# Three groups of mixer steps traced one to three steps later in a decoder layer on one core

## The chip, the cores and the metric

The kernel runs on one core of a Trainium2 chip. The metric is the device time of one execution in microseconds (us); of several executions the median is taken. The engines are TensorE (PE, with its weight loads as PEld), VectorE (DVE), ScalarE (ACT), GpSimd (POOL), and SyncE (SP), whose queue issues the weight loads from memory.

## What is computed

One decoder layer in float32 for 256 tokens of width 2048. A feed-forward block comes first and last; between them stand the mixer, which this document is about, and a cross-attention into 256 memory vectors. The mixer of the reference, cut to what matters:

```python
h = rms_norm(x, norm_g)
p = h @ w_in
q, k, v, p_rwkv, gates = jnp.split(p, c, axis=-1)
y_attn = sliding_window_attention(q, k, v, sinks)          # 16 heads, 4 key heads of 64
y_rwkv = rwkv7_time_mix(p_rwkv, ...)                       # 16 heads of 64, a scan over time
gate_attn, gate_rwkv = jnp.split(jax.nn.sigmoid(gates), 2, axis=-1)
merged = gate_attn * (y_attn @ w_proj_attn) + gate_rwkv * (y_rwkv @ w_proj_rwkv)
return x + merged @ w_out
```

and in `rwkv7_time_mix` the two sigmoids over 1024 columns that the change concerns:

```python
w_log = -softplus(-(w0 + jnp.tanh(xw) @ w2)) - 0.5
a = jax.nn.sigmoid(a0 + xa @ a2)
```

## The kernel before

**Products.** Every weight matrix is read once, in units of 256 rows by up to 512 columns. Each unit is split on ACT (L299, the high part) and DVE (L300, the rest), and a product of 256 tokens with it is three matmuls for every 128 rows of the matrix and every 128 tokens (`multiply`, L336 to L338). `product` (L312) walks through the units of one column block; units are loaded by SP's queue (L287) four units ahead and split two units ahead.

**Steps.** All other work of the mixer consists of Python generators that are put into queues (`Interleave`, L51 on: "const", "feat", "attn", "ew", "chain", "norm", "mem"). After the six matmuls of one unit for one half of the tokens, `product` calls `bg.tick()` (L324), and a tick advances the first task of every queue by one `yield` (two tasks in "attn", three in "chain"). So a `yield` is the unit of distance: a piece of work behind it is traced one step, which is six product matmuls, later. `idle(n)` yields n times. A task that needs another's result waits, step by step, until a name is put into `bg.seen`. A product whose left operand isn't traced yet goes on ticking without matmuls (L320). The tile framework then makes each engine's order out of the traced order, and puts in the waits; each engine works its queue in that order.

**Around the change.** The products of the mixer follow one another: queries (two blocks), keys and values, the small columns (288 wide), the RWKV keys (two), four times gate and attention projection, receptances and values (two of each), four gates, four blocks of the RWKV projection, four of the output product.

- `keys_values` (L515 on): transposes the keys (L347), copies them to `kd` (L521), and moves one half of them to the other partitions by two DMAs on POOL's queue (L522). Next step: the values are copied (L525). After `idle(2)` the name "kv" is seen. The eight `attend` tasks wait for it, two at a time; the first thing they do is the scores (L542) from `kd`, into two of the three PSUM banks named `mm`. The last one lets "attn" be seen.
- `decay_and_rate` (L644 on) waits for "attn". It loads `wa` on POOL's queue (L648, L649), and then, in four groups, makes four matmuls each (L661; the profile shows two records for each, 32 in all) into two `mm` banks, and four sigmoids on ACT (L668), with a `yield` between groups. Then come scans and exponentials, and "decay" is seen. Behind it in the same queue "ew" stand `removal_keys` for two halves (L717, L754 on PE), `substitute` (a loop of 31 small DVE steps; its input `dl` is read by SP's queue, L775), and `receptances` and `values` for two halves (L835, L843). These set off the `pair` tasks of the queue "chain" (L893 to L960), and those the `finish` tasks (L985, L994), which split the second branch into `yr`.
- `merged` (L1033 on): after each block of the RWKV projection, DVE multiplies the gate in (L1045) and POOL adds the two branches (L1046), one instruction for each half of the tokens, into `ml`. The task then waits one `yield`, transposes `ml` on PE (L347, two groups of four) and splits it (L352, L353) into the left operand `mt` of the output product.

Large tiles of the mixer share a ring of 20 buffers (`t4`); the PSUM has three banks for products (`acc`), three `mm` and two `tr`.

Of the kernel before, what the change touches and what calls it, by code (L numbers as in the profile page):

```python
# [120 lines left out]
def decoder_layer(ctx: ExitStack, tc: tile.TileContext, a: dict, out: bass.AP):  # L121
# [24 lines left out]
    def mm():  # L146
        return ps.tile([P, 512], F32, tag="mm", name="mm")
# [4 lines left out]
    def wait_for(name):  # L152
        while name not in bg.seen:
            yield

    def idle(n):
        for _ in range(n):
            yield
# [181 lines left out]
    def feat(tok, cols):  # L340


        b = tr()
        for i, col in enumerate(cols):
            for t in range(2):
                o = (2 * i + t) * P
                pe.transpose(b[:, o : o + P], tok[:, t, col : col + P], ident[:])  # L347
        return b[:].rearrange("p (c t) -> p c t", c=2)

    def split(x: Act, c, n, src):  # L350

        act.copy(x.at(0, c, n), src)  # L352
        dve.tensor_tensor(x.at(1, c, n), src, f32(x.at(0, c, n)), ALU.subtract)  # L353
        x.done |= set(range(c, c + n))
# [124 lines left out]
    with tc.tile_pool(name="mx", bufs=1, reuse_waits="tile") as sp:  # L479
        aligned(sp)  # L480

        def t4(name, shape=(P, 4, T), dt=F32):
            return sp.tile(list(shape), dt, tag="t4", name=name, bufs=N4)
# [31 lines left out]
        def keys_values():  # L515

            b = feat(tok_kv, C4[:2])
            v = kd[:].rearrange("p (c e) t -> p c e t", e=2)
            for e in range(2):
                r, o = slice(64 * e, 64 * e + 64), slice(64 - 64 * e, 128 - 64 * e)  # L520
                act.copy(v[r, :, e, :], b[r])  # L521
                pool.dma_start(v[o, :, e, :], v[r, :, e, :])  # L522
            yield
            for t in range(2):
                dve.tensor_copy(vt[:, t, :], tok_kv[:, t, KV_W : 2 * KV_W])  # L525
            yield from idle(2)
            bg.seen.add("kv")

        bg.spawn("feat", keys_values())
        ya = act_tiles("ya", 2)  # L530
        sink4 = sinks[:].rearrange("p (k c e) -> p k e c", k=4, c=2)
# [101 lines left out]
        def halves(x):  # L633
            return x[:].rearrange("p c (b t) -> p (c b) t", b=2)
# [9 lines left out]
        def decay_and_rate():  # L644
            yield from wait_for("small")
            yield from wait_for("attn")
            wa = t4("wa", (P, RW))
            pool.dma_start(wa[0:64, :], W["rwkv_w2"])  # L648
            pool.dma_start(wa[64:128, :], W["rwkv_a2"])  # L649
            act.activation(xwa[0:64, :], xwa[0:64, :], AF.Tanh)  # L650
            act.activation(xg, xg, AF.Sigmoid)
            yield
            for h in range(2):
                cs.append(t4("cs"))
                aa.append(t4("aa"))
                for q in (0, 2):
                    b = [mm() for _ in range(2)]
                    for i in range(2):
                        for e in range(2):
                            r, c = slice(64 * e, 64 * e + 64), (4 * h + q + i) * P  # L660
                            pe.matmul(  # L661
                                b[e][:, i * T : (i + 1) * T], wa[r, c : c + P], xwa[r, :],
                                start=True, stop=True,
                            )
                    for i in range(2):
                        for e, (dst, bias) in enumerate(((cs[h], w0), (aa[h], a0))):
                            c = 4 * h + q + i
                            act.activation(  # L668
                                dst[:, q + i, :], b[e][:, i * T : (i + 1) * T], AF.Sigmoid,
                                bias=bias[:, c : c + 1],  # L670
                            )
                    yield
            for h in range(2):
                for c in range(4):
                    dve.tensor_tensor_scan(
                        cs[h][:, c, :], keep2, cs[h][:, c, :], 0.0, ALU.mult, ALU.add
                    )
                    if c % 2:
                        yield
                c3 = halves(cs[h])  # L680
                mid = stat.tile([P, 8], F32, tag="mid", name="mid")
                dve.tensor_copy(mid[:], c3[:, :, 63])
                dve.tensor_tensor(
                    c3, c3, mid[:].unsqueeze(2).to_broadcast([P, 8, P]), ALU.subtract
                )
                dec.append(stat.tile([P, 4], F32, tag="dec", name="dec"))
                dve.tensor_tensor(dec[h][:], cs[h][:, :, 127], mid[:, 1:8:2], ALU.add)
                yield
                act.activation(dec[h][:], dec[h][:], AF.Exp, scale=-DECAY)

                ee.append(t4("ee", (P, 8, P)))
                e0.append(stat.tile([P, 8], F32, tag="e0", name="e0"))
                act.activation(e0[h][:], mid[:], AF.Exp, scale=DECAY)
                act.activation(ee[h][:], c3, AF.Exp, scale=-DECAY)
                yield
                act.activation(cs[h][:], cs[h][:], AF.Exp, scale=DECAY)
                yield
            bg.seen.add("decay")

        bg.spawn("ew", decay_and_rate())  # L700
        kt = []

# [328 lines left out]
        mt = act_tiles("mt", 4)  # L1031

        def merged(m, n):  # L1033
            yield
            for q in (0, 2):
                split(mt, 4 * n + q, 2, feat(m, C4[q : q + 2]))
                yield

        for n in range(4):
            g, m = t4("gl", (P, 2, 512)), t4("ml", (P, 2, 512))  # L1040
            pool.dma_start(g[:], blk(grd, n))
            pool.dma_start(m[:], blk(md, n))
            pr = product(yr, W["w_proj_rwkv"])
            for t in range(2):
                dve.tensor_tensor(g[:, t, :], pr[t][:], g[:, t, :], ALU.mult)  # L1045
                pool.tensor_tensor(m[:, t, :], g[:, t, :], m[:, t, :], ALU.add)  # L1046
            bg.spawn("feat", merged(m, n))
# [166 lines left out]
```

## Time and profile before

| what | value |
|---|---|
| median of 3 runs (lowest, highest) | 2328.53 us (2326.44, 2334.17) |
| the profiled execution | 2327.99 us |
| its span, first to last instruction | 2326.3 us |
| mean granted TensorE clock | 0.998 |
| PE busy in 700 to 800 us | 100.00 of 100 |
| PE busy in 800 to 900 us | 97.34 of 100, clock 0.98 |
| PE busy in 900 to 1000 us | 99.72 of 100 |
| PE busy in 1300 to 1400 us | 96.80 of 100 |
| DVE busy, whole span | 1259.5 us |
| ACT busy, whole span | 1078.2 us |

The mixer runs from about 754 us to 1600 us. The keys' task is found at 816 us, the sigmoids at 879 to 889, the sum of the branches at 1350 to 1396. A wait is shown as the idle time of an engine before an instruction, together with what released it.

### The profile page before, as it was taken

To read this page: it belongs to the slowest core of one execution; us is meant where nothing else is said; L and a number is where in the kernel's file an instruction comes from. 1 tells how busy PE (TensorE), PEld (TensorE's weight loads), DVE (VectorE), ACT (ScalarE), POOL (GpSimd) and SP (SyncE) were. 2 spreads that over 40 slices of the span, in tenths; PEclk is the share of its full clock that TensorE was granted. 3 is DMA by queue.
4 is the path that set the end of the run, shared out by engine and by line. 5 is a ranking of instruction groups with operands and counts; after the bars stand their busy time and mean duration, and the time that the engine had idled before them with its cause. 6 is when DMAs were issued, how large, how long until landed. Compare 5 with 4: busy or idle time off the path is not lost.

```text
span 2326.3 us, 27347 instructions
## 1 busy us (share of the span) xinstructions
PE 2303.9 (99%) x10853; PEld 1895.5 (81%) x10853; DVE 1259.5 (54%) x1395; ACT 1078.2 (46%) x1425; POOL 130.3 (6%) x192
## 2 busy tenths in 40 slices
PE   8999999999999999999999999999999999999998
PEld 7888888888888877888888878888888888888887
DVE  4545544554556477795444556555545544554545
ACT  5444344434445477444344446455444344434444
POOL 1000000000000000201220030001000000000001
PEclk9999999999999999999999999999999999999999
DMA  8555655556554544676432576648555555555553
GB/s 291 181 196 184 198 186 194 184 196 194 186 189 152 173 129 145 197 230 206 123 103 88 174 246 217 199 156 297 195 184 194 189 196 184 196 185 195 193 187 127
DMA packets 219856, 432.71 MB, mean 186 GB/s; under 512 B 14267, under 2 KB 17040, under 8 KB 219728
## 3 DMA queue, kind: packets, MB, share of 16 engines
q1 hardware_dynamic: 211520, 405.58, 53.3%
q0 software_dynamic: 8176, 25.38, 3.4%
q8 instruction: 85, 1.39, 0.2%
q14 instruction: 43, 0.35, 0.0%
q10 hardware_dynamic: 32, 0.01, 0.0%
HBM read 417.56 MB, written 13.11 MB: 185 GB/s over the span
## 4 chain that ended last, share of the span: by engine, by line
PE 93%; issue 4%; DVE 1%; DMA 1%; ACT 1%; POOL 1%; SPq 0%; POOLq 0%; ACTq 0%
PE acc L336 28%; PE acc L338 28%; PE acc L337 28%; PE tr L347 2%; PE mm L924 1%; PE tr L893 1%; POOL ml L1046 0%; PE mm L542 0%; DMA raw<-in_ffn_w_gate_dram 0%; PE tr L911 0%; ACT hi L299 0%; PE tr L994 0%; PE tr L907 0%; PE tr L581 0%; PE tr L589 0%
## 5 line engine op out<-in xcount | busy, mean ns | idle before, releaser
L300 DVE TENSOR_TENSOR lo<-raw,hi 128x1024 fp32r<-128x1024 f32 (+1 forms) x769 | 942.1, 1226 | 956.3 <-ACT hi L299 955.6
L299 ACT CAST hi<-raw 128x1024 fp32r<-128x1024 f32 (+1 forms) x769 | 805.5, 1048 | 1066.1 <-PE acc L338 1028.8
L336 PE MATMUL acc<-hi,xhi 128*128 128x512 f32 (+1 forms) x2016 | 798.7, 396 | 0.4 <-ACT xhi L373 0.4
L337 PE MATMUL acc<-lo,xhi 128*128 128x512 f32 (+1 forms) x2016 | 785.4, 390 | 0.0
L338 PE MATMUL acc<-hi,xlo 128*128 128x512 f32 (+1 forms) x2016 | 784.6, 389 | 0.0
L336 PEld LDWEIGHTS acc<-hi,xhi 128*128 128x128 f32 x2016 | 379.7, 188 | 80.3 <-issue 3.4
L338 PEld LDWEIGHTS acc<-hi,xlo 128*128 128x128 f32 x2016 | 379.1, 188 | 79.5 <-issue 1.0
L337 PEld LDWEIGHTS acc<-lo,xhi 128*128 128x128 f32 x2016 | 379.9, 188 | 78.0 <-issue 3.6
L336 PE MATMUL acc<-hi,hhi 128*128 128x512 f32 x704 | 275.5, 391 | 0.0
L338 PE MATMUL acc<-hi,hlo 128*128 128x512 f32 x704 | 274.2, 389 | 0.0
L337 PE MATMUL acc<-lo,hhi 128*128 128x512 f32 x704 | 274.0, 389 | 0.0
L338 PEld LDWEIGHTS acc<-hi,hlo 128*128 128x128 f32 x704 | 132.1, 188 | 27.5
L337 PEld LDWEIGHTS acc<-lo,hhi 128*128 128x128 f32 x704 | 132.2, 188 | 27.2
L336 PEld LDWEIGHTS acc<-hi,hhi 128*128 128x128 f32 x704 | 132.2, 188 | 26.8
L336 PE MATMUL acc<-hi,mthi 128*128 128x512 f32 x128 | 51.2, 400 | 0.0
L338 PE MATMUL acc<-hi,mtlo 128*128 128x512 f32 x128 | 50.1, 392 | 0.0
L337 PE MATMUL acc<-lo,mthi 128*128 128x512 f32 x128 | 49.9, 390 | 0.0
L1167 POOL TENSOR_TENSOR x<-x,fin 128x512 f32<-128x512 f32 x6 | 8.9, 1505 | 695.4 <-ACT junk L1165 695.4
L470 POOL DMA_DIRECT2D x1d<-x x4 | 3.0, 744 | 710.4 <-DVE x L427 710.4
L415 ACT ACTIVATE hb<-acc,rs 128x512 f32<-128x512 f32 x44 | 30.2, 690 | 19.5 <-PE acc L338 19.5
L352 ACT CAST hhi<-tr 128x512 fp32r<-128x512 f32 x44 | 25.7, 583 | 16.3 <-PE tr L347 16.3
L373 ACT ACTIVATE xhi<-tr,gains 128x256 fp32r<-128x256 f32 x48 | 22.0, 470 | 21.8 <-DVE xlo L374 16.1
(289 smaller groups left out, 1632.7 us busy)
## 6 DMA issues: line engine op xcount, KB each, us to landing
raw<-in_ffn_w_up_dram SPq DMA_DIRECT2D x88, 1024.0 KB, 5.1
raw<-in_ffn_w_down_dram SPq DMA_DIRECT2D x88, 1024.0 KB, 5.0
raw<-in_ffn_w_gate_dram SPq DMA_DIRECT2D x86, 1024.0 KB, 5.1
raw<-in_w_in_dram SPq DMA_DIRECT2D x136, 512.0 KB, 3.5
raw<-in_w_out_dram SPq DMA_DIRECT2D x32, 512.0 KB, 4.6
raw<-in_w_proj_attn_dram SPq DMA_DIRECT2D x16, 512.0 KB, 3.8
raw<-in_w_proj_rwkv_dram SPq DMA_DIRECT2D x16, 512.0 KB, 5.5
raw<-in_w_cross_kv_dram SPq DMA_DIRECT2D x16, 512.0 KB, 3.6
```

Source lines behind the costliest of these rows:

```text
L299: act.copy(hi[:, s], raw[:, s])
L300: dve.tensor_tensor(lo[:, s], raw[:, s], f32(hi[:, s]), ALU.subtract)
L336: pe.matmul(o, xh, hi[:, i, :], start=k + i == 0, stop=False)
L337: pe.matmul(o, xh, lo[:, i, :], start=False, stop=False)
L338: pe.matmul(o, xl, hi[:, i, :], start=False, stop=k + i == nk - 1)
L347: pe.transpose(b[:, o : o + P], tok[:, t, col : col + P], ident[:])
L352: act.copy(x.at(0, c, n), src)
L373: last = act.activation(self.x.at(0, c), b[:, j, :], AF.Copy, scale=g)
L415: act.activation(hb[:, t, :], pg[t][:], AF.Silu, scale=norm.r[t])
L893: pe.matmul(b[e][:, m * P : (m + 1) * P], x1[r, j, cs_], x2[r, j, cs_], start=True, stop=True,)
L924: pe.matmul(vb[:, o : o + P][:, r], lhs(e), rhs[:, r], start=first and e == 0, stop=True, **ek,)
L1167: pool.tensor_tensor(xs, xs, fin[:, n * 512 : (n + 1) * 512], ALU.mult)
```

## The change

Three places wait longer, counted in steps, before the work behind them is traced. Nothing that is computed changes, and no instruction is added or removed.

```diff
@@ keys_values
             for t in range(2):
                 dve.tensor_copy(vt[:, t, :], tok_kv[:, t, KV_W : 2 * KV_W])
-            yield from idle(2)
+            yield from idle(3)
             bg.seen.add("kv")
@@ decay_and_rate, behind each of the four groups
                             act.activation(
                                 dst[:, q + i, :], b[e][:, i * T : (i + 1) * T], AF.Sigmoid,
                                 bias=bias[:, c : c + 1],
                             )
-                    yield
+                    yield from idle(2)
@@ merged
         def merged(m, n):
-            yield
+            yield from idle(4)
             for q in (0, 2):
                 split(mt, 4 * n + q, 2, feat(m, C4[q : q + 2]))
                 yield
```

The first place moves the heads' tasks by one step, the second puts one more step behind each of the four groups, and the third moves the transposes of each block by three steps.

## The prediction

> **What bounds the kernel.** I read the page first: busy time by engine, then the chain that ended last.
>
> ```profile
> PE 2303.9 (99%) x10853; PEld 1895.5 (81%) x10853; DVE 1259.5 (54%) x1395; ACT 1078.2 (46%) x1425; POOL 130.3 (6%) x192
> ...
> PE 93%; issue 4%; DVE 1%; DMA 1%; ACT 1%; POOL 1%; SPq 0%; POOLq 0%; ACTq 0%
> ```
>
> TensorE (PE) is busy for 99% of the span, and 93% of the chain is its own instructions. No change in the order of work can win more than PE's idle time: 2326.3 - 2303.9 = 22.4 us, plus whatever its instructions lose by being slow. Then I read the busy time by stretch. Of the 22.4 us, 7.4 lie in the first 100 us and 8.6 after 1700 us, where this change touches nothing. 6.4 us are left in the mixer: 2.7 between 800 and 900, 0.3 between 900 and 1000, 0.2 between 1200 and 1300, 3.2 between 1300 and 1400. The list of what PE waited for (total, times, longest) names them:
>
> ```profile
> PE tr L347 <- POOL ml L1046: 3.1, 3, 1.0
> PE mm L542 <- DMA kd<-kd: 1.3, 1, 1.3
> PE tr L581 <- DVE s L575: 0.6, 1, 0.6
> PE mm L661 <- ACT aa L668: 0.5, 1, 0.5
> ...
> PE mm L661 <- ACT cs L668: 0.3, 1, 0.3
> ```
>
> The three edits sit on these rows: the DMA of the keys, the sigmoids, the sum of the branches. So each edit is priced from its own place in the timeline (columns: start, length, engine, line, operation, count, idle time before it). One step is six 128x512 matmuls at 0.23 us from start to start, 1.37 us.
>
> **The branches' sum (L1033 on, three steps later).** The second of the four column blocks:
>
> ```profile
> 1366.04 0.27 PE L347 MATMUL tr<-ident,ml 128*128 128x128 f32 x1
> ...
> 1367.35 0.55 PE L347 MATMUL tr<-ident,ml 128*128 128x128 f32 x3 [1.04 <-POOL ml L1046]
> ...
> 1367.66 0.48 PE L336 MATMUL acc<-hi,yrhi 128*128 128x512 f32 x1
> ```
>
> The second transpose needs the second half of the sum, which POOL ends at 1367.3. From the first transpose to the next product matmul pass 1.62 us; the undisturbed four at 1369.12 are followed by it after 0.35. Lost: 1.27 us, in three blocks; the first block (1353.93 to 1354.57) loses 0.29. Together 4.1 us. Two steps separate product and transposes today; with five there are 5 x 1.37 = 6.9 us, and POOL is done 4.2 us after the product (1363.1 to 1367.3), so 2.7 us are to spare. Gain **4.1 us**. The task then takes seven steps of a product's eight, so it doesn't pile up; the last block is split in step 6 of the output product, which reads it from its thirteenth step on. The `ml` buffers are held three steps (4.1 us) longer: the loads of `mem` queued on POOL at 1394 to 1397 need about 8.1 us (as `ml`'s did), and PE reads them at 1419.9, which leaves some 15.
>
> **The sigmoids (L661 to L672, two steps apart in place of one).** PE's rows, without the product matmuls between them:
>
> ```profile
> 879.04 1.13 PE L661 MATMUL mm<-xs,wa 64*128 64x256 f32 x4
> 880.99 1.14 PE L661 MATMUL mm<-xs,wa 64*128 64x256 f32 x8
> 883.04 2.22 PE L661 MATMUL mm<-xs,wa 64*128 64x256 f32 x12 [0.25 <-ACT cs L668]
> 885.81 1.13 PE L661 MATMUL mm<-xs,wa 64*128 64x256 f32 x4 [0.55 <-ACT aa L668]
> 887.29 1.13 PE L661 MATMUL mm<-xs,wa 64*128 64x256 f32 x4
> ```
>
> Four groups of eight records; each group needs two of the three `mm` banks, which ACT empties by four sigmoids of some 0.37 us (1.5 us, beside a 1.05 us cast): more than one step, less than two. So the groups come apart. Besides the waits of 0.8, a torn group is slow: eight records with both halves of the array alternating took 1.07 us (880.99 to 882.06), four alone also 1.06. From 878.72 to 889.16 lie ten product matmuls (2.3 us), so the 32 records cost 8.1 us; as four whole groups they would cost 4 x (1.07 + 0.2 for changing over) = 5.1. The gain is 3.0 if all four come whole; if all are torn into fours, 8 x 1.26 = 10.1, a loss of 2.0. I take **2.0**: nearest to whole groups, because two steps free the banks, less one torn group, since the first is torn today with all banks free.
>
> **The keys' DMA (L526, one step later).** Columns of the second view: busy time and count of PE, PEld, DVE, ACT, POOL, then granted clock and DMA.
>
> ```profile
> 818.91 0.71 PE L542 MATMUL mm<-kd,qt 64*128 64x128 f32 x4
> ...
> 821.60 2.42 PE L542 MATMUL mm<-kd,qt 64*128 64x128 f32 x12 [1.25 <-DMA kd<-kd]
> ```
> ```profile
> 820.00:822.00 2.00, 0.75 (x8) 0.52 (x8) 0.75 (x2) 0.99 (x1) 0.00 (x0) 1.00 0.90 228
> 822.00:824.00 2.00, 2.00 (x12) 1.16 (x8) 1.54 (x4) 0.00 (x0) 0.00 (x0) 0.54 0.78 232
> 824.00:825.00 1.00, 1.00 (x5) 1.00 (x5) 1.00 (x3) 0.00 (x0) 0.00 (x0) 0.50 0.23 88
> 825.00:826.00 1.00, 1.00 (x8) 1.00 (x7) 1.00 (x4) 0.86 (x5) 0.00 (x0) 0.71 0.00 0
> ```
>
> The wait costs 1.25 us, and behind it the clock falls to half: 0.46 x 2 + 0.5 + 0.29 = 1.7 us of full clock. But a step here is short: the product is 288 wide, six matmuls take 0.79 us. And PE's queue isn't the traced order: four records, four product matmuls, then twelve. One step later, six product matmuls come ahead of the four records, and the twelve may follow directly, as the order put them where it took the DMA for done. PE then reaches them at 820.4 instead of 820.2, and the data still lands at 821.6. Gain 0.2 at that end; 0.7 if four matmuls again lie between; nothing if the order is unmoved. I take **0.2**, wait left about 1.1. The clock: the 1.25 us wait had it halved, the three waits of 1.04 at `ml` had not (1.00 from 1366 to 1370). 1.1 is nearer to these: **1.7** goes. The ends for the whole edit are 0 and 3.0.
>
> [...]
>
> **What the moved steps drag along.** The heads' tasks start one step later, the decay task five (one, and four from the sigmoids); behind it in one queue come the removal keys, the substitution, receptances and values, then the pair chains: up to 5 x 1.37 = 6.9 us later. At the end that is covered: the last split of the second branch runs at 1319.6, its product begins at 1340.3. POOL's `rb` memset waited 4.0 us for a buffer; its loads land by 1215 and PE first reads that half at 1246. SP's queue: the reads of `ld` (L775) wait 4.9 us for POOL's writes at 977 to 983 with weight loads behind them; five steps later they still do, 4.9 + 2.4 for the issue = 7.3 us, against four loaded units of 2.7 us each. VectorE (DVE) is fullest there, 80 of 100 us between 900 and 1000. I charge nothing: today's waits in 900 to 1300 are 0.5 us in all, so a new position should cost about as little; between -1 and the last rival's price.
>
> **Sum.** 4.1 + 2.0 + 0.2 + 1.7 = 8.0 us. The profiled execution took 2327.99 us (span 2326.3, 1.7 around it), 0.5 under the median of 2328.53. Forecast 2327.99 - 8.0 = **2320.0**, 0.37% under the median. About 0.3% (7.0 us, 2321.5) is what a measurement can tell from no change.
>
> **Rivals.**
> *The half-clock window stays.* For: the wait remains about 1.1 us, between 1.04 (no halving) and 1.25 (halving). 2327.99 - 6.3 = 2321.7. [...]
> *The sigmoid groups stay torn.* Only the waits of 0.8 go, or nothing: 2321.2 to 2324 with or without the window. For: the first group is torn today with no bank in the way.
> *It doesn't do what it says.* The PE order is made from more than the traced order, so moved steps may land in the same place: 2328. Against: the `ml` transposes stand exactly two steps behind the product, as traced.
> *Slower: the waits move.* The removal keys and values give PE sixteen groups (two at each of L717, L754, L835, L843, for two halves), each behind a DVE or ACT result. If the new position makes each wait as long as the longest in-order loss seen here, 1.27 us, that is 20 us: 2340. It outweighs the gain of 8.0 from the seventh group on; half of them give 2330. For: DVE's 80%, and the 0.3 us at L754 today. Against: those sixteen have 0.3 us in all.
>
> **Chances.** Forecast 0.46; window stays 0.22 (0.04 of it below the 0.3% line); torn groups 0.08; no effect 0.04; waits move 0.20 (0.14 of it beyond 0.3%). So faster 0.50, same 0.36, slower 0.14. The range reaches down to 2315 (all upper ends: 4.1 + 3.0 + 3.0 = 10.1, about 2318; the -1 of the drag, and its scatter) and up to 2333, into the last rival.
>
> **What would show it.** Right: no `ml` wait in PE's list; L661 in whole groups of eight without idle time; the clock at 1.00 throughout 820 to 826; idle time of the mixer 6.4 down to some 2. Wrong: L542 still waiting for `kd` by a microsecond with the clock at half; new PE rows on L717, L754, L835 or L843; a wait of casts (L299) on weight loads behind L775; idle time at the second branch's product.

## The result and the profile after

The changed kernel takes 2325.35 us (median of 22 runs, 2323.16 to 2330.8) against 2329.14 (22 runs, 2326.28 to 2334.17): a ratio of 0.9985, 95% interval 0.9979 to 0.9991. By the ratio it is 3.5 us faster, where 8.0 were forecast. By the prediction's own line of 0.3% (7.0 us) that is no change, for which it had a chance of 0.36. The profiled execution was one of its long ones (2329.57 us, span 2327.9, the second longest of 22), so its rows tell where time went, and the medians how much.

Page of the changed kernel, busy time and chain:

```profile
PE 2303.2 (99%) x10853; PEld 1893.5 (81%) x10853; DVE 1261.3 (54%) x1395; ACT 1078.0 (46%) x1425; POOL 130.9 (6%) x192
...
PE 92%; issue 4%; DMA 2%; DVE 1%; ACT 1%; POOL 0%; SPq 0%; ACTq 0%; POOLq 0%; DVEq 0%
```

The list of what PE waited for (total us, times, longest), from its third row:

```profile
PE acc L337 <- DVE lo L300: 2.1, 3, 1.3
PE mm L542 <- DMA kd<-kd: 1.9, 1, 1.9
PE acc L336 <- ACT hi L299: 1.2, 1, 1.2
PE mm L661 <- ACT cs L668: 0.9, 1, 0.9
PE tr L347 <- DVE x L1066: 0.9, 2, 0.6
PE tr L581 <- DVE s L575: 0.8, 2, 0.5
```

The three waits for the `ml` sum are gone. The other two targets aren't: the keys' DMA costs 1.9 us in place of 1.3, the sigmoids still 0.9. And waits are new, those of the products themselves for split weights (L336, L337) above all. In all, PE's idle time from the first `tok` transpose to the memory product rose from 6.4 to 9.0 us.

**The sum** went as forecast. Four transposes in a row, and the next product matmul 0.35 us behind the first of them:

```profile
1362.46 0.60 PE L347 MATMUL tr<-ident,ml 128*128 128x128 f32 x4
1362.81 0.48 PE L336 MATMUL acc<-hi,yrhi 128*128 128x512 f32 x1
```

**The sigmoids**: of the four groups of eight only the last is whole; the others come as 4, 8, 8 and 4.

```profile
886.82 1.13 PE L661 MATMUL mm<-xs,wa 64*128 64x256 f32 x4
...
888.77 1.14 PE L661 MATMUL mm<-xs,wa 64*128 64x256 f32 x8
...
890.83 1.79 PE L661 MATMUL mm<-xs,wa 64*128 64x256 f32 x8 [0.91 <-ACT cs L668]
...
892.81 0.70 PE L661 MATMUL mm<-xs,wa 64*128 64x256 f32 x4
...
895.88 1.13 PE L661 MATMUL mm<-xs,wa 64*128 64x256 f32 x8
```

They also start at 886.8, 7.8 us later than before, though the heads were moved by one step.

**The keys.** Timeline and busy time by stretch (last three columns: granted clock, DMA share, GB/s):

```profile
819.58 0.48 PE L542 MATMUL mm<-kd,qt 64*128 64x128 f32 x2
821.98 3.09 PE L542 MATMUL mm<-kd,qt 64*128 64x128 f32 x14 [1.92 <-DMA kd<-kd]
```
```profile
820.00:822.00 2.00, 0.08 (x3) 0.02 (x2) 0.35 (x1) 0.00 (x0) 0.00 (x0) 1.00 0.88 199
822.00:824.00 2.00, 2.00 (x12) 1.34 (x13) 1.44 (x3) 0.00 (x0) 0.00 (x0) 0.62 0.93 299
824.00:826.00 2.00, 2.00 (x8) 1.33 (x6) 1.58 (x4) 0.00 (x0) 0.00 (x0) 0.50 0.01 5
826.00:828.00 2.00, 2.00 (x10) 2.00 (x9) 1.72 (x5) 1.14 (x2) 0.00 (x0) 0.50 0.00 0
```

PE stops after two records in place of four, the data lands 0.4 us later than before (4.5 us from issue, before 4.0), and the half clock lasts 6.8 us in place of 3.4.

To add up a profile without the chance of the clock, I split PE's course by four marks: the first `tok` transpose (771), the first matmul with `yrhi`, the first with `mehi`, the last with `hhi`. From the first stretch I take half of the time that the clock records at half.

| kernel (its profile) | to the first `yr` product | at half clock | first stretch at full clock | second branch to memory product | rest |
|---|---|---|---|---|---|
| before | 569.3 | 3.4 | 567.6 | 145.3 | 831.3 |
| changed | 573.9 | 10.2 | 568.8 | 142.5 | 831.1 |

The sum's stretch gained 2.8 us, the rest is level, and the stretch that the other two edits touch lost 1.2 at full clock, and another 3.4 to the clock. Half of the time at half clock is more than such a time really cost (1.3 us for 3.4); the next section puts this right.

### The profile page after: what moved, and what is told of

It reads as the page before. It is cut to its first block, busy times and chain, and to the rows that moved or that the text cites. A ratio compares the mean times of both kernels' runs of the same rounds, so it can differ in the third digit from the quotient of the medians.

```text
span 2327.9 us, 27346 instructions
## 1 busy us (share of the span) xinstructions
PE 2303.2 (99%) x10853; PEld 1893.5 (81%) x10853; DVE 1261.3 (54%) x1395; ACT 1078.0 (46%) x1425; POOL 130.9 (6%) x192
## 4 chain that ended last, share of the span: by engine, by line
PE 92%; issue 4%; DMA 2%; DVE 1%; ACT 1%; POOL 0%; SPq 0%; ACTq 0%; POOLq 0%; DVEq 0%
PE acc L336 28%; PE acc L337 28%; PE acc L338 28%; PE tr L347 2%; PE mm L924 1%; PE tr L893 1%; DVE lo L300 0%; PE mm L542 0%; DMA raw<-in_ffn_w_gate_dram 0%; DMA raw<-in_w_out_dram 0%; ACT hi L299 0%; PE tr L911 0%; DMA raw<-in_w_in_dram 0%; ACT s L567 0%; PE tr L994 0%
## 5 line engine op out<-in xcount | busy, mean ns | idle before, releaser
L300 DVE TENSOR_TENSOR lo<-raw,hi 128x1024 fp32r<-128x1024 f32 (+1 forms) x769 | 943.2, 1227 | 956.0 <-ACT hi L299 955.4
L299 ACT CAST hi<-raw 128x1024 fp32r<-128x1024 f32 (+1 forms) x769 | 805.4, 1048 | 1061.2 <-PE acc L338 1027.8
L336 PE MATMUL acc<-hi,xhi 128*128 128x512 f32 (+1 forms) x2016 | 799.5, 397 | 1.4 <-ACT hi L299 1.2
L337 PE MATMUL acc<-lo,xhi 128*128 128x512 f32 (+1 forms) x2016 | 787.2, 390 | 2.1 <-DVE lo L300 2.1
L336 PEld LDWEIGHTS acc<-hi,xhi 128*128 128x128 f32 x2016 | 380.3, 189 | 82.9 <-issue 5.4
L337 PEld LDWEIGHTS acc<-lo,xhi 128*128 128x128 f32 x2016 | 380.7, 189 | 81.1 <-DVE lo L300 3.3
L336 PE MATMUL acc<-hi,hhi 128*128 128x512 f32 x704 | 275.5, 391 | 0.0
L337 PE MATMUL acc<-lo,hhi 128*128 128x512 f32 x704 | 274.0, 389 | 0.0
L336 PEld LDWEIGHTS acc<-hi,hhi 128*128 128x128 f32 x704 | 132.2, 188 | 26.9
L337 PEld LDWEIGHTS acc<-lo,hhi 128*128 128x128 f32 x704 | 132.2, 188 | 26.9
L336 PE MATMUL acc<-hi,mthi 128*128 128x512 f32 x128 | 51.2, 400 | 0.0
L337 PE MATMUL acc<-lo,mthi 128*128 128x512 f32 x128 | 49.9, 390 | 0.0
```

The source lines that it names most:

```text
L299: act.copy(hi[:, s], raw[:, s])
L300: dve.tensor_tensor(lo[:, s], raw[:, s], f32(hi[:, s]), ALU.subtract)
L336: pe.matmul(o, xh, hi[:, i, :], start=k + i == 0, stop=False)
L337: pe.matmul(o, xh, lo[:, i, :], start=False, stop=False)
```

## The experiments

Every ratio is against the kernel before. The stretches are those of the table above.

**One edit at a time.** The first three kernels hold one hunk each of the change, the fourth the second and third:

```diff
# e1, e4                                  # e2, e4
-            yield                        -                    yield
+            yield from idle(4)           +                    yield from idle(2)
# e3
-            yield from idle(2)           (in front of bg.seen.add("kv"))
+            yield from idle(3)
```

> Only the sum's edit (transposes of the merged branches three steps later). Theory, from the trace after: this edit alone carries the whole gain; the ml wait (three of 1.04 us, 4.1 us with what lies around them) goes and nothing else moves, so about 4.1 us less than before (0.18%), and the keys' DMA wait stays at about 1.25 us. Rival: the three edits share the gain, and this one's freed time is partly lost at the output product, so 1 to 3 us less.

> Only the sigmoids' edit (one more step behind each of the four groups). Theory: the groups save 1 us or less, and the four-step shift of the removal keys and the substitution puts SP's four reads of ld behind three weight loads in place of two, so weights come late near 1000 us: PE waits there 1 to 2 us and may lose another 1.7 us to a half-clock window; net 0 to 3 us slower than before. Rival (the prediction): whole groups, 2.0 us faster, nothing near 1000 us.

> Only the keys' edit (heads one step later). Theory: four records and their wait are moved so that PE comes to the DMA's data with less other work ahead, wait 1.9 us in place of 1.25, and the half clock lasts two windows of 3.4 us in place of one; 1 to 2.5 us slower than before. Rival (the prediction): wait about 1.1, clock at full, 1.9 us faster.

> The change without the keys' edit: sum and sigmoids. Theory: the sum's 4.1 us less the sigmoids' loss of 0 to 3, so 1 to 4 us under before; PE idle near 1000 us on weights as in the profile after, keys' DMA wait 1.25 us with one half-clock window. Rival: 6.1 us under before, with no wait near 1000 us.

| kernel | median us | ratio (95%) | first stretch | at half clock | at full clock | second stretch |
|---|---|---|---|---|---|---|
| sum | 2323.71 | 0.9980 (0.9971, 0.9988) | 568.0 | 0 | 568.0 | 142.1 |
| sigmoids | 2326.4 | 0.9993 (0.9984, 1.0002) | 569.0 | 6.8 | 565.6 | 146.5 |
| keys | 2336.0 | 1.0029 (1.0018, 1.0041) | 578.4 | 10.2 | 573.3 | 145.2 |
| sum + sigmoids | 2323.68 | 0.9977 (0.9968, 0.9986) | 573.3 | 17.1 | 564.8 | 141.9 |

The sum alone gains 4.7 us by the ratio, as much as the whole change or more. In its second stretch 3.2 us of that can be seen, and the runs with a recorded mean clock of 0.999 differ by 3.0 (2323.6 against 2326.5). Sum and sigmoids gain 5.4, between what I expected and the rival.

**What a clock window costs.** A window is here a time in which the profile records half of the clock. Where two executions have the same order on PE, the start of the same matmul can be compared. The window of 3.4 us at 822 puts the kernel before 1.3 us behind the sum alone, not 1.7. The 6.8 us at 857 put the sigmoids' kernel 3.1 us behind sum and sigmoids, and the 17.1 us from 1137 put the latter 7.3 us behind the former, not 8.5. Priced so, the first stretch at full clock is 568.0 for the kernel before and for the sum, 565.9 for the sigmoids, and 566.0 for sum and sigmoids. So the 564.8 of the table is 1.2 too low, and differences of less than about 1 us between two values of that column can't be relied on.

The sigmoids' edit thus gains 2.0 to 2.1 us in the first stretch, alone and beside the sum. Alone it loses 1.2 in the second stretch, where a fourth wait for `ml` came up (4.2 us in all), and by the ratio its gain isn't certain. Where I expected it to lose near 1000 us, PE has no wait.

**Where the 2.0 us lie.** The same product matmul can be timed in both kernels at points where both have done the same other work. Against the sum alone, the sigmoids' kernel is 3.0 us behind at 875 us (its clock window), 2.4 behind at 904, 3.5 behind at 1114 and 1.1 behind at 1306. So the four groups of the sigmoids win 0.6 us, the stretch behind them loses 1.1, and the `pair` tasks win 2.4. Of these, L893 (192 records) takes 21.9 us from start to start in the kernel before and 19.1 with the sigmoids' edit. A group of L893 is twelve records, six for either half of the array. Before, only 4 of the 16 groups come whole with the halves alternating. Others are torn, as here by a product matmul, and either half takes 0.86 to 0.87 us:

```profile
1204.07 0.49 PE L893 MATMUL tr<-at,aa 64*128 64x128 f32 x2
1204.40 0.38 PE L893 MATMUL tr<-rt,aa 64*128 64x128 f32 x2
1204.62 0.38 PE L893 MATMUL tr<-rt,kk 64*128 64x128 f32 x2
1204.94 0.49 PE L336 MATMUL acc<-hi,xhi 128*128 128x512 f32 x1
1205.36 0.49 PE L893 MATMUL tr<-at,aa 64*128 64x128 f32 x2
1205.68 0.38 PE L893 MATMUL tr<-rt,aa 64*128 64x128 f32 x2
1205.91 0.38 PE L893 MATMUL tr<-rt,kk 64*128 64x128 f32 x2
1206.22 0.50 PE L337 MATMUL acc<-lo,xhi 128*128 128x512 f32 x1
```

With the sigmoids' edit 8 of the 16 come whole, and a whole one takes 0.87 us:

```profile
1134.06 0.49 PE L893 MATMUL tr<-at,aa 64*128 64x128 f32 x4
1134.39 0.39 PE L893 MATMUL tr<-rt,aa 64*128 64x128 f32 x4
1134.61 0.39 PE L893 MATMUL tr<-rt,kk 64*128 64x128 f32 x4
1134.93 0.50 PE L336 MATMUL acc<-hi,xhi 128*128 128x512 f32 x1
```

The changed kernel has 8 whole groups too, and so has the last kernel below, which moves what follows by four steps without the sigmoids' edit. So this gain comes from the four steps by which the `pair` tasks stand later, not from the distance between the groups of the sigmoids.

**What the keys' edit costs.** Alone it costs 6.8 us, much more than the 1 to 2.5 I expected. Beside the sigmoids it costs 3.9 us at full clock: with its windows priced by matching matmuls (4.0 us, against the kernel with the reads of `ld` moved, below) the changed kernel's first stretch is 569.9, against 566.0.

Why so much, the keys' kernel's ACT queue shows:

```profile
890.91 0.47 ACT L668 ACTIVATE aa<-mm,rv 128x256 f32<-128x256 f32 x1
...
893.09 1.28 ACT L693 ACT_TABLE_LOAD   x1
...
894.39 0.21 ACT L693 ACTIVATE e<-mid 128x8 f32<-128x8 f32 x1
...
894.61 1.28 ACT L668 ACT_TABLE_LOAD   x1
895.91 0.47 ACT L668 ACTIVATE cs<-mm,rv 128x256 f32<-128x256 f32 x1
...
897.17 1.26 PE L661 MATMUL mm<-xs,wa 64*128 64x256 f32 x4 [2.91 <-ACT cs L668]
```

A tiny exponential of the first half (L693) came between the sigmoids; each turn of kind costs a table load of 1.28 us, and the last four records wait 2.9 us for a bank. In the kernel before, the sigmoids run with one load, and the next comes behind the last of them:

```profile
877.74 1.28 ACT L668 ACT_TABLE_LOAD   x1
...
889.90 1.28 ACT L689 ACT_TABLE_LOAD   x1
```

**The reads of `ld` off SP's queue**, in the changed kernel:

```diff
-                nc.sync.dma_start(dl[q], ld[q, :, q].rearrange("t h s -> h t s"))
+                pool.dma_start(dl[q], ld[q, :, q].rearrange("t h s -> h t s"))
```

> The changed kernel, with the substitution's four reads of ld taken from SP's queue to POOL's, so that no weight load stands behind their wait. Theory: PE's waits on the split weights near 1000 us (1.2 + 0.5 us in the trace after) and the half-clock window behind them go, 1.7 to 3.4 us less than the changed kernel, so about 2322 to 2323.5; the wait at 904 us (1.3 us) stays. Rival: those waits come from VectorE, which is full there; then they stay and the time is that of the change, 2325.

In the changed kernel, SP waits for the writes of `ld`, and behind it the casts of the weights stop for 7.15 us, and PE with them (first SP's list of waits, then rows of the timeline):

```profile
SPq L775 <- DMA ld<-lt: 4.8, 1, 4.8
```
```profile
1000.12 2.00 ACT L299 CAST hi<-raw 128x1024 fp32r<-128x1024 f32 x2 [7.15 <-PE acc L338]
...
1001.22 0.73 PE L336 MATMUL acc<-hi,xhi 128*128 128x512 f32 x2 [1.18 <-ACT hi L299]
...
1002.48 0.50 PE L337 MATMUL acc<-lo,xhi 128*128 128x512 f32 x1 [0.53 <-DVE lo L300]
```

With the reads on POOL's queue, PE is busy for all 120 us from 980 to 1100 (118.29 in the changed kernel), and its list keeps only the other waits:

```profile
PE mm L542 <- DMA kd<-kd: 1.6, 1, 1.6
PE acc L337 <- DVE lo L300: 1.6, 2, 1.3
PE mm L661 <- ACT cs L668: 0.9, 1, 0.9
```

Median 2324.59, ratio 0.9981 (0.9972, 0.9991); first stretch 567.3 with no half clock, 2.6 under the changed kernel's 569.9: 2.2 for the waits near 1000 us (1.7 idle, and slower matmuls behind them), and 0.3 by which the keys' wait was shorter. The row of the casts names a PE matmul as what ended their idle time; but with nothing moved except the reads the idle time goes, so SP's queue was the cause there. The intervals of the two ratios overlap; it is the trace that shows it. The wait of 1.3 at 904 stayed, as the theory said.

**The place alone**: the decay task starts one step later, the heads stay.

```diff
             yield from wait_for("attn")
+            yield
             wa = t4("wa", (P, RW))
```

> Sum and sigmoids, with the decay task held back by one more step at its start, and the heads where they were: all that follows the decay stands at the changed kernel's step (five later), but the heads don't. Theory (what the keys' edit loses is lost behind the decay task, by its new place): the waits at 904 and 1000 us come back without the keys' edit, time 2325 to 2326. Rival (it is lost in the heads and the keys' wait, 800 to 890 us): no such waits, time as without the step, 2323 to 2324.

Each is half right. The waits near 1000 us came back (0.9 on L299 and 0.5 on L300), so they belong to the place of the removal keys and the substitution. The wait at 904 didn't, and the time stayed at 2323.29, ratio 0.9971 (0.9961, 0.9982). The first stretch is 569.4; its window of 6.8 us cost 2.8 by matching matmuls, which leaves 566.6, 0.6 above the 566.0 without the step, and 0.6 is what the keys' wait is longer. So the later place of the decay task costs nothing on balance: it loses 2.0 near 1000 us and has the wait at L907 at 0.2 in place of 1.4. What the keys' edit costs beyond its longer wait lies for the most part in the heads and sigmoids: 2.8 us, there by 907 us. Here the keys' wait was 1.9 us with a landing of 4.6, though nothing ahead of it was changed: the 1.9 of the changed kernel isn't the edit's doing alone, the landing varies by half a microsecond.

**The keys' DMA on another queue**, and **four steps in place of one**, both with sum and sigmoids:

```diff
-                pool.dma_start(v[o, :, e, :], v[r, :, e, :])      # e7
+                act.dma_start(v[o, :, e, :], v[r, :, e, :])
-            yield from idle(2)                                    # e8
+            yield from idle(6)
```

> Sum and sigmoids, the keys' edit undone, and the two DMAs of the keys issued by ACT's queue in place of POOL's. Theory: the wait before the scores is the landing of these DMAs behind POOL's two issues of 0.6 us each (4.0 us from issue to landing); from a hardware queue they land a microsecond or more sooner, so the wait of 1.25 falls to 0.3 or less: 1 to 2 us under sum and sigmoids alone (2321.7 to 2322.7). Rival: the landing is as late (the queue isn't the cause), wait and time unchanged at 2323.7.

> Sum and sigmoids, and the keys' edit made four steps in place of one: the scores stand about 3.2 us later than before, behind the landing of the DMA. Theory: the wait for kd is gone (0 in place of 1.9), but the heads, the decay task and what follows stand eight steps later, and waits come up elsewhere in 850 to 1010 us; what is won at the keys (1.25 and a clock window) is given back, 2322 to 2327. Rival (the keys' wait is the whole loss of that edit): 2 us or more under sum and sigmoids alone, 2321 or less.

On ACT's queue the landing took 4.3 us and the wait 1.2 (sum and sigmoids, on POOL's: 4.0 and 1.3): the queue isn't the cause, that theory falls (2323.74, ratio 0.9977, 0.9968 to 0.9986). For the microsecond of the theory, the profile of before has only transfers of 8 KB from memory: 2.8 us on ACT's queue, 5.3 to 6.0 on POOL's. The time is that of sum and sigmoids, but not for the same reasons: the heads' order moved, a wait of 1.2 for L575 came up, and the first stretch is 568.3 against 566.0, while 9 of 11 runs have a recorded mean clock of 0.999. With four steps the wait nearly goes, 0.4 with a landing of 5.3:

```profile
PE mm L661 <- ACT cs L668: 1.1, 1, 1.1
...
PE mm L542 <- DMA kd<-kd: 0.4, 1, 0.4
```

2320.92 us (2320.14 to 2321.39), ratio 0.9962 (0.9950, 0.9975), first stretch 565.2. At full clock that is 0.8 better than the 566.0 without any edit of the keys; the rest of what four steps win is the clock: all five runs have a recorded mean clock of 0.999. Here my expectation was wrong, and the rival right.

**ACT's order held**, by putting exponentials behind the last sigmoid `sg`:

```diff
-                act.activation(e0[h][:], mid[:], AF.Exp, scale=DECAY)
+                with tc.issue_after(sg.ins):
+                    act.activation(e0[h][:], mid[:], AF.Exp, scale=DECAY)
```

(the same for `dec`; in the third kernel below for `ee` and `cs` too).

> Only the keys' edit, and ACT's order held: the small exponentials of the decay task (e0, dec) are put behind the last sigmoid. Theory: the keys' edit alone is 7 us slower (2336) since an exponential of the first half came between the sigmoids, with two table loads of 1.28 us on ACT, so that PE waited 2.9 us for a bank and lost a clock window behind it; held back, that wait goes and 3 to 6 us with it: 2330 to 2333. Rival (the loss is in the heads' new order and the keys' wait, 815 to 875 us): 2335 to 2336 still.

> The changed kernel with the same order on ACT. Theory: the two table loads between the sigmoids (897 to 904 us) go, and with them the late casts and PE's wait of 1.3 us on the split weights at 904; 1 to 2.5 us under the changed kernel, 2323 to 2324.5, with the waits near 1000 us as they were. Rival (VectorE is what is late at 904): the wait stays, 2325.

> All findings together: sum, sigmoids, keys by four steps, all exponentials behind the last sigmoid, and the reads of ld on POOL's queue. Theory: each was a loss of its own, so under the 2320.9 of the four-step kernel by 0.5 to 2 us: 2319 to 2320.5. Rival (every repair moves the list that the order is made from, and opens a wait elsewhere): 2321 to 2324.

> Sum and keys by four steps, without the sigmoids' edit. Theory (the sigmoids' edit is worth some 1.6 us wherever it stands): 2322 to 2323. Rival (it only matters for where the groups fall, and its extra steps cost as much as they save): 2320 to 2321, as with it.

The keys' edit alone with the order held: one table load at 882.6, none between the sigmoids, PE's longest wait there 0.9 in place of 2.9, ratio 1.0011 (1.0002, 1.0020) in place of 1.0029. PE's order is the same in both, and 3.5 us of what lies between the two profiles come at the sigmoids: 2.0 of wait, the rest the clock window at 898 that is gone. So the loads were some 4 of its 6.8 us, and the theory holds. What is left, 571.7 against 568.0 in the first stretch, is idle time: PE has 4.2 us more of it between 815 and 980 us, which I didn't take apart.

The changed kernel with the order held settles nothing: another exponential (now L696) took the place of the held ones, the two loads stayed (895.9 and 898.3), and so did the wait of 1.3 at 904; 2326.0, ratio 0.9989 (0.9980, 0.9997). The loads alone don't make that wait: sum and sigmoids have two loads between the sigmoids and no such wait, and the last kernel below has a wait of 1.7 at 901 without any load between them. What does stays open.

All findings together give the fastest kernel of the study: **2318.83 us**, ratio **0.9957** (0.9944, 0.9969), with one table load at 883.8 and a first stretch of 564.2. Without the sigmoids' edit, four steps at the keys give 2323.23, ratio 0.9981 (0.9973, 0.9990), against 0.9962 with it; the intervals just touch (0.9973 to 0.9975), and the difference is in the direction of the theory.

## Why the prediction came out as it did

The direction was right and the time lay inside the range, with less than half of the forecast gain, and the parts agree much less than the total. Two of the prediction's own signs of being wrong appeared: L542 still waiting for `kd` with the clock at half, and casts held up behind L775. Two of its rivals held: the window stayed, and the groups stayed torn. In the two profiled executions, at full clock and with the windows priced by matching matmuls, in us won:

| part | forecast | measured |
|---|---|---|
| keys, heads and sigmoids, to 907 us | 2.2 | -3.2 |
| from there to 1120 us | 0 | -1.9 |
| the `pair` tasks | 0 | 3.2 |
| the sum (second stretch) | 4.1 | 2.8 |
| half clock | 1.7 | -2.7 |
| together | 8.0 | -1.8 |

- *The sum, 4.1 us.* Right. The second stretch is 4.1 us shorter in three of the kernels that have it, and 2.7 to 3.8 in the others; the changed one (2.8) lost the rest mostly to a wait of the next task for L1066 (0.9 us).
- *The sigmoids, 2.0 us.* The size came out by luck. The groups were to come whole, and the first three are torn as before; the spacing took away the wait of 0.55 at the fourth, and won 0.6 at this place. (By the prediction's own rows, 3.0 less 1.3 for one torn group is 1.7, not 2.0.) The other gain lies in the `pair` tasks, from torn groups of L893 that became whole: the mechanism that I had priced for L661, at a place where I had put nothing. The edit also brought two more table loads on ACT along, and, alone or beside the sum, a wait of 1.4 us at 1135 to 1138 (L907).
- *The keys, 0.2 us.* This is the step that failed. I priced the wait alone, and the edit's cost lies in what its one step does to the order behind it: 3.9 us beside the sigmoids, 6.8 alone. Alone, the table loads that come between the sigmoids are some 4 of that, shown by holding ACT's order. Beside the sigmoids, 0.6 are the keys' longer wait and 2.8 lie in the heads and sigmoids; what makes these isn't shown. "PE's queue isn't the traced order" stood in my text, but I drew it on for one place only.
- *The clock, 1.7 us.* Wrong. I reasoned that a wait of about 1.1 would not halve the clock; the wait stayed at 1.3 to 1.9 in the kernels with this edit, and in this trace the half clock came back, twice as long. The step also took one execution's window for a fixed price, and 1.3 of the 1.7 is what it cost. By the mean clock recorded with each of 77 runs of before, 29 have 0.999 and a median of 2326.7, and 32 have 0.997 and 2330.4: the clock differs from run to run, and these two groups lie 3.7 us apart. The changed kernel has 0.999 in 9 of its 22 runs, about as often.
- *The drag, nothing.* Wrong in both directions. SP's reads of `ld`, a place that I had named, cost 2.2 us: I set the block of 7.3 us against four loaded units of 2.7 and found it covered; but the loads behind the reads were issued from 992.8 us on, and the casts stood still for 7.15 us. And the `pair` tasks, five steps later, win 3.2. The other covers held (chain, `rb`, `ml`).
- The rival "the waits move" was to act on L717, L754, L835 and L843. Those rows stayed at 0.2. Waits did move, but to ACT's table loads and SP's queue, where I had no price in the sum.

The profiled execution of the changed kernel was 1.6 us longer than that of before, which the table explains. At full clock the change wins 0.9 in it; the runs with a recorded mean clock of 0.999 differ by 2.4 (2324.3 against 2326.7), and the medians of all runs give 3.5. What lies between these I can't take apart.

## What to carry to other kernels

A step moved in a list from which a tool makes each engine's order is a new list: price not only the wait that it should cover, but look at every in-order queue behind it for what may now come between, on ACT above all for functions that need another table (1.28 us a load here). Where a wait is longer than the step by which the waiting work is moved (1.25 us against 0.79), moving it once does little but stir the order; moved far enough it nearly went (0.4), and all five runs had a recorded mean clock of 0.999. Small matmuls that use one half of the array each are worth following through such a move: whether other matmuls fall between the two halves made 2.4 to 3.2 us here, more than 200 us behind the edit. And an edit that is measured only together with others may be a loss that they hide: the change without its first hunk is as fast or faster (0.9977 against 0.9985, with intervals that overlap). And a total near the forecast can be the sum of errors: time the same instruction in both kernels at several places before calling a term right.

## What the runs showed of the hardware

In these profiles the length of PE's idle time doesn't settle whether the clock halves. One and the same wait of 1.3 us for the keys had 3.4 us at half clock behind it in the profile of before, and none in that of the sum alone, where the clock is 1.00 in every stretch read from 815 to 2300 us; with the DMA on ACT's queue the wait was 1.2, and 9 of 11 runs had a mean clock of 0.999. In the profile of sum and sigmoids, 17.1 us at half clock from 1136.7 (mean clock 0.96 from 1100 to 1320 us) follow a wait of 1.4 us at 1135, in a stretch of many small matmuls. The same wait stands in that of the sigmoids alone, where the clock is 1.00 from 1100 to 1320 us; in that profile 6.8 us at half clock come at 857 (0.91 from 835 to 875 us), and the wait just ahead of them is one of 0.6 us at 855, which the kernel before has too, without a window. Nor is the loss half of the window: 3.4 us at half clock cost 1.3, and 17.1 us cost 7.3. Why one wait had a half clock behind it and another of the same length none isn't shown.

Six records of L893 for one half of the array took 0.86 to 0.87 us (before, 1204 to 1206 us), and twelve with both halves alternating 0.87 (sigmoids alone, 1134 us).

The keys' DMA between partitions took 3.9 to 5.6 us from issue to landing in the profiles of this study, with the same data and, but for one kernel, on the same queue.
